# A two-layer decoder trunk on one core: shorter Pool instructions, one head's rotation on DVE, deferred work spread out, two reordered joints

## The chip, the cores and the metric

The kernel runs on 1 core of one Trainium2 chip. The metric is device time in microseconds; 3 runs of the kernel before have a median of 1151.61 us (1150.71 to 1155.07). PE is TensorE, DVE is VectorE, ACT is ScalarE, POOL is GpSimd, SP is SyncE, which issues the DMAs.

## What is computed

The input x is 512 tokens of 1024 features in fp32. Each of two layers computes

```python
n = rmsnorm(h, attn_norm[l])
u, v_sgu, q, k, v_att = split(n @ w_in[l])                # 512 columns each
y_sgu = gelu(u) * (causal_128x128(w_s) @ rmsnorm_by_group(gelu(v_sgu)) + b_s)
y_att = differential_attention(rope(q), rope(k), v_att)   # 4 heads, two softmaxes each, normed
h = h + concat(y_sgu, y_att) @ w_out[l]
h = h + (silu(conv3(n2 @ w_up_gate)) * conv3(n2 @ w_up_value)) @ w_down[l]   # n2 = rmsnorm(h, ffn_norm[l])
```

and a last rmsnorm follows. The FFN has 2816 gate and 2816 value features; conv3 is a causal convolution of width 3 along the tokens.

## The kernel before, in words

**Products.** Features lie on the 128 partitions, the 512 tokens along the free dimension. Each fp32 operand is split into a high part (a cast to fp32r) and a low part (the rest, by a subtraction), and each product is three matmuls: high by high, high by low, low by high. A step of `feat_gemm` (L235) takes one of eight input blocks for two output banks, 6 matmuls of 128x512; `tok_gemm` (L252) does the same with tokens as rows, 12 matmuls of 128x256.

**Weights.** `block` (L156) keeps two blocks ahead (AHEAD): SP issues the DMA of a 128x1024 block into `raw`, ACT casts it into `wh`, and DVE or Pool subtracts (`wl <- raw, wh`, L169 and L170). Pool does nearly all blocks of w_in and w_out and every third of the FFN, DVE the others. Three buffers each hold `raw`, `wh` and `wl`, so the cast of a block waits until TensorE has used up an earlier one. A new block is asked for at every fourth step.

**Order.** From the input products to the end of the attention and of w_out, each engine's instructions are pinned to program order (`pin`, L107). In the FFN they are not; the tile framework orders them. TensorE's products are written as generators; `run(steps, n)` (L261) advances a product by n steps and after each takes one piece of DVE, ACT and Pool work from the queue `due`.

**Input products.** `products` (L770) goes in each layer through gate values, queries and keys of heads 0 and 1, attention values of heads 0 and 1, then queries, keys and values of heads 2 and 3, the gates u, and the first part of w_out. `rope` (L491) rotates two heads: `turn` shuffles on DVE (sh), multiplies by cosines on DVE (t1), multiplies by sines on Pool and adds on Pool; `part` splits the result (ACT cast, DVE subtraction), giving k_0h and k_0l for head 0. The last DVE piece before the attention is `small` (L460): the mixing factor lambda, `nlam`.

**Attention.** 16 units (4 heads by 4 query tiles, L848 to L903), each passing through scores, mask and minimum on DVE (`s<-sc,mask` and `mn`), exponentials on ACT, difference on DVE (`s<-s,cf,s`), transposes (`at`), a split (`aTh` on ACT, `aTl` on DVE), values (`av`) and their sum on DVE (`o<-av`). Units are pipelined: unit i's scores stand beside unit i-1's transposes and unit i-2's values. During the first eight units, three steps of the input products run per unit. Score banks and transpose banks are two each, so scores wait for a mask reduction and `at` or `av` for an earlier `aTl` or `o`. Temporary tiles (t1, sh, score tiles, gate values) share a pool `tp` of 12 buffers. In layer 0 the second gate's norm work is not in `due`: all of it but the first two pieces (squares, sums, square root, normalisations, splits) goes into `later` (L768, L777) and then the masking and split of the spatial weights (`spatial`, L478, L834); up to two entries are taken at each unit's end (L899). Layer 1 has an empty `later`.

**Towards the FFN.** After the attention, w_out's output blocks 0 to 3 (`pairs`) lack their last two inputs; `late` (blocks 4 and 5) begins with six steps, then the last head's output is transposed and split (`end.out_turn`, `out_high`, `out_low`), then `project_last` adds input 6, one step of `late`, `project_last` adds input 7 (L918 to L929). Then come a weight block, the residual of blocks 0 to 3 (`hT<-wo,hT`, which frees their banks, and the next norm's scaled pieces gh_f and gl_f and squares), the rest of `late`, and blocks 6 and 7 in the freed banks. In the FFN's first pair, six of eight gate steps run, then `norm.sums` (L414): TensorE transposes the summed squares acc_f into ss_f, DVE reduces them and takes the reciprocal square root by 11 small operations after one scaling; then the last two gate steps, one value step, `norm.rows` (L424), which transposes the root into rows and copies them to rstd on ACT, and the rest.

Of the kernel before, what the change touches and what calls it, by code (L numbers as in the profile page):

```python
# [13 lines left out]
F32 = mybir.dt.float32  # L14
# [8 lines left out]
S = 512  # L23
# [46 lines left out]
def trunk(ctx: ExitStack, tc, a, out):  # L70
# [50 lines left out]
    pe, act, dve, gps = Ordered(nc.tensor), Ordered(nc.scalar), Ordered(nc.vector), Ordered(nc.gpsimd)  # L121
# [21 lines left out]
    for l in range(DEPTH):  # L143
        specs += [a["w_in"][l, c] for c in range(20)]
        specs += [a["w_out"][l, c] for c in range(8)]
        for half in range(2):
            lo = 0 if half == 0 else FF_SPLIT[0] // 2
# [8 lines left out]
    def block(i):  # L156
        while len(loaded) <= min(i + AHEAD[0], len(specs) - 1):
            j = len(loaded)
            n = specs[j].shape[-1]
            if j >= len(specs) - 6:  # L160
                loaded.append(kept(j, n))
                continue
            raw = wp.tile([P, 1024], F32, tag="raw", name=f"raw{j}")[:, :n]
            h = wp.tile([P, 1024], F32R, tag="wh", name=f"wh{j}")[:, :n]
            lo = wp.tile([P, 1024], F32R, tag="wl", name=f"wl{j}")[:, :n]
            (sync if j < 6 else nc.sync).dma_start(out=raw, in_=specs[j])
            act.copy(h, raw)
            i_l = j % (len(specs) // DEPTH)
            eng = gps if (j > 6 and i_l != 27 if i_l < 28 else j % 3 == 1) else dve  # L169
            eng.tensor_sub(lo, raw, h.bitcast(F32))  # L170
            loaded.append((h, lo))
        return loaded[i]

# [87 lines left out]
    def run(steps, n=None):  # L261

        for i, _ in enumerate(steps):
            if due:
                due.popleft()()
            if i + 1 == n:
                break


    due = deque()  # L270
# [178 lines left out]
    for l in range(DEPTH):  # L449
# [28 lines left out]
        def spatial():  # L478
            gps.affine_select(
                out=wsp, in_=wsp, compare_op=ALU.is_ge, fill=0.0, base=0,  # L480
                pattern=[[0, NG], [1, P]], channel_multiplier=-1,
            )
            act.copy(ws_h, wsp)
            gps.tensor_sub(ws_l, wsp, ws_h.bitcast(F32))

        qs, ks = [None] * NH, [None] * NH
# [4 lines left out]
        def rope(banks, store, at, name):  # L491

            t1, sh = [None, None], [None, None]

            def turn(j):
                sh[j] = tmp(f"{name}{l}_{at + j}sh")
                dve.stream_shuffle(sh[j], banks[j], SHUF)
                t1[j] = tmp(f"{name}{l}_{at + j}t1")
                dve.tensor_mul(t1[j], banks[j], Cr)
                gps.tensor_mul(sh[j], sh[j], Sr)  # L500
                gps.tensor_add(t1[j], t1[j], sh[j])

            def part(j):
                store[at + j] = split(f"{name}{l}_{at + j}", t1[j])

            return [partial(turn, 0), partial(turn, 1), partial(part, 0), partial(part, 1)]

        def query_banks(hp):
            return [mm_bank(f"q{2 * hp + j}_{l}") for j in range(2)]
# [6 lines left out]
        def keys(hp):  # L516
            banks = [mm_bank(f"k{2 * hp + j}_{l}") for j in range(2)]
            yield from feat_gemm(banks, xs)
            due.extend(rope(banks, ks, 2 * hp, "k"))

        def values(hp):
            banks = [mm_bank(f"va{b}_{hp}_{l}") for b in range(2)]
# [241 lines left out]
            g, q = gate_work(0, vb), rope(qb, qs, 0, "q")  # L764
            due.extend([nothing] * 4 + g[:2] + q[:2] + g[2:4] + [lambda: [f() for f in g[4:7]]] + q[2:] + g[7:])


        later = deque()  # L768

        def products():  # L770
            if l == 0:
                yield from both_first()
                banks = value_banks(1, sc_bank)
                yield from tok_gemm(banks, xs)
                g = gate_work(1, banks)
                due.extend(g[:2])
                later.extend(g[2:])  # L777
            else:
                yield from gate_values(0)
                yield from queries(0)  # L780
                yield from gate_values(1)
            yield from keys(0)
            yield from values(0)
            yield from queries(1)
            yield from keys(1)
            yield from values(1)
            yield from gates(0)
            yield from gates(1)
            yield from project()
# [15 lines left out]
        def project_last(k):  # L805
            for c in range(2):
                feat_step(pairs[c], mixed[k], final[0], (2 * c + k - KD + 2) * 256, False, k == KD - 1)
# [3 lines left out]
        steps = products()  # L811
        if l == 0:
# [7 lines left out]
            Cr, Sr = rotary_turn()  # L820
        else:
# [7 lines left out]
            Cr, Sr = fslot(f"Cr{l}"), fslot(f"Sr{l}")  # L829
            dve.tensor_mul(Cr, CT, norm.rstd)  # L830
            dve.tensor_mul(Sr, ST, norm.rstd)
        run(steps, 28 - (22 if l == 0 else 15))
        if l == 0:
            later.append(spatial)  # L834
        else:
            spatial()
        run(steps, 12)
        flush()
# [9 lines left out]
        for i in range(len(todo) + 2):  # L848
            u0 = None
            u1, u2, u3 = at(i - 1), at(i - 2), at(i - 3)  # L850
            ot = at(i - HEAD_LATE)
            if ot and ot.qt < NT - 1:
                ot = None
            if ot:
                ot.out_turn()
                ot.out_high()
            if u3:
                u3.out()
            if biased:
                biased.pop()()  # L860
            if i < len(todo):
                h, qt = todo[i]
                if qt == 0:
                    head = Head(h)
                units.append(Unit(h, qt, head))
                u0 = units[i]
                u0.scores()
            if ot:
                ot.out_low()
            run(steps, 1)  # L870
            if u1:
                u1.turn()
            if u0:
                u0.exps()
            elif i == len(todo):
                gelu(0)
                gelu(1)
            if u3:
                u3.out_square()
                if u3.qt == NT - 1:  # L880
                    u3.out_rms()
            run(steps, 1)
            if u1:
                u1.high()
            if u0:
                u0.difference()
            if u1:
                u1.low()
            n3 = at(i - 4)
            if n3 and n3.qt == NT - 1:  # L890
                n3.out_norm()
            if u2:
                u2.values()
            if i in MIX_AT:
                biased.append(mix(MIX_AT.index(i)))
            for _ in range(min(2, len(later))):
                later.popleft()()
            if i < 8:
                run(steps, 1)  # L899
            if i == len(todo):  # L900
                gated(0)
                gelu(2)
                gelu(3)  # L903
# [14 lines left out]
        late = [sc_bank(f"wo{4 + j}_{l}") for j in range(2)]  # L918
        more = feat_gemm(late, mixed)
        AHEAD[0] = 1  # L920
        run(more, 6)
        AHEAD[0] = 2
        end.out_turn()
        end.out_high()
        end.out_low()
        mixed[-1] = ya[3]
        project_last(KD - 2)
        run(more, 1)
        project_last(KD - 1)  # L929
        flush()  # L930

# [40 lines left out]
        for half in range(2):  # L972
            nf = FF_SPLIT[half]
            acts = []
            for pr in range(nf // 2):
                f = f0 + 2 * pr
                gb = [mm_bank(f"g{f + j}_{l}") for j in range(2)]
                steps = feat_gemm(gb, xs)
                vb = [mm_bank(f"v{f + j}_{l}") for j in range(2)]
                more = feat_gemm(vb, xs)  # L980
                if half == 0 and pr == 0:
                    run(steps, 6)
                    norm.sums()
                    run(steps)
                    run(more, 1)
                    norm.rows()
                run(steps)
                gs = []
                for j in range(2):
                    c = conv(gb[j], f + j, f"cg{l}_{f + j}")  # L990
                    act.activation(c, c, AF.Silu)
                    gs.append(c)
                run(more)
                for j in range(2):
                    c = conv(vb[j], NF + f + j, f"cv{l}_{f + j}")
                    dve.tensor_mul(c, c, gs[j])
                    acts.append(split(f"ac{l}_{f + j}", c, gps))
            f0 += nf
            if half == 1 and not last_layer:
                norm = Norm(f"a{l + 1}", C_AN + (l + 1) * KD)  # L1000
            for c in range(2 if half == 1 and last_layer else 4):
                banks = [mm_bank(f"dn{half}_{2 * c + j}_{l}") for j in range(2)]
                run(feat_gemm(banks, acts))
                if half == 1 and last_layer:

                    block(len(specs) - (4 if c == 0 else 1))
                for j in range(2):
                    m = 2 * c + j
                    dve.tensor_add(hT[m], banks[j], hT[m])
                    if half == 1 and not last_layer:  # L1010
                        norm.feed(m)
# [169 lines left out]
```

## Time and profile before

| what | value |
|---|---|
| median of 3 runs | 1151.61 us |
| the profiled execution's own time | 1152.52 us |
| its span, first to last instruction | 1150.8 us |
| mean granted TensorE clock | 0.993 |
| busy: PE, PEld | 97%, 81% |
| busy: DVE, ACT, POOL | 61%, 41%, 34% |
| chain that ended last: PE, DVE, ACT, POOL | 84%, 7%, 3%, 3% |

The execution's time is the span and 1.7 us around it. PEld is TensorE's weight load, which lies beside its matmuls. The span falls into layer 0's input products and attention (to about 172 us), w_out and the FFN (to 577), the same for layer 1 (to 735 and 1133), and the last norm. In the views below, start and length are in us, "out<-in" are the program's tile names without numbers of buffers, and what stands in brackets is the idle time of that engine just before and who ended it. L119 is the line of the wrapper through which pinned instructions go, so tile names tell them apart.

### The profile page before, as it was taken

Reading aid. Unit: us, or ns where it says so; the run is one execution under the profiler, and the core shown is the slowest. Engines: PE = TensorE matmul, PEld = TensorE weight load, DVE = VectorE, ACT = ScalarE, POOL = GpSimd, SP = SyncE. Lnnn points to the kernel's source line nnn. Section 1 sums busy time; section 2 is a strip of 40 time slices with the busy share of each in tenths; the row PEclk is TensorE's granted clock in tenths of the full one; section 3 lists DMA queues with packets and bytes.
Section 4 is the critical chain, followed back from the end, with each engine's and each line's share of the span. In section 5 each row is a group of like instructions: output and inputs, shape, how many; then the busy total and the mean of one; then the engine's idle time right before and its main releaser. Section 6 shows DMA issues by size and latency. Waiting matters only on the chain.

```text
span 1150.8 us, 14822 instructions
## 1 busy us (share of the span) xinstructions
PE 1119.3 (97%) x5637; PEld 937.6 (81%) x5637; DVE 697.3 (61%) x1267; ACT 477.4 (41%) x810; POOL 393.0 (34%) x303
## 2 busy tenths in 40 slices
PE   9998999999999999999999999999999999999996
PEld 7976887788888888888899688877888888888886
DVE  6778874866663236674357777757666522565634
ACT  6544552454442134343343554544444421344351
POOL 0556223522422013323456652252323311322351
PEclk9999999999999999999999999999999999999998
DMA  8221122223233332233232211222333333232222
GB/s 268 74 74 55 56 65 74 92 92 103 84 107 92 110 92 92 92 101 92 101 106 81 85 59 53 73 74 95 108 92 99 96 99 93 90 110 92 81 85 73
DMA packets 34215, 105.24 MB, mean 91 GB/s; under 512 B 4064, under 2 KB 8544, under 8 KB 34144
## 3 DMA queue, kind: packets, MB, share of 16 engines
q1 hardware_dynamic: 33712, 104.27, 28.6%
q8 instruction: 44, 0.72, 0.3%
q14 instruction: 27, 0.22, 0.1%
q10 hardware_dynamic: 432, 0.03, 0.0%
HBM read 102.19 MB, written 2.10 MB: 91 GB/s over the span
## 4 chain that ended last, share of the span: by engine, by line
PE 84%; DVE 7%; ACT 3%; POOL 3%; issue 2%; DVEq 0%; POOLq 0%; ACTq 0%
PE v L119 21%; PE g L119 20%; PE dn L119 18%; PE wo L119 7%; PE u L119 4%; PE vs L119 3%; PE dl L119 3%; PE q L119 2%; PE k L119 1%; ACT wh L119 1%; PE sc L119 1%; PE av L119 1%; PE mx L119 1%; DVE s L119 1%; POOL wl L119 1%
## 5 line engine op out<-in xcount | busy, mean ns | idle before, releaser
L119 POOL TENSOR_TENSOR wl<-raw,wh 128x1024 fp32r<-128x1024 f32 (+1 forms) x96 | 230.1, 2398 | 580.4 <-ACT wh L119 570.5
L119 ACT CAST wh<-raw 128x1024 fp32r<-128x1024 f32 (+1 forms) x192 | 194.2, 1014 | 376.3 <-issue 189.4
L119 DVE TENSOR_TENSOR wl<-raw,wh 128x1024 fp32r<-128x1024 f32 (+1 forms) x96 | 123.3, 1284 | 135.9 <-ACT wh L119 135.8
L119 PE MATMUL g<-gh_f,wh 128*128 128x512 f32 x352 | 137.8, 391 | 0.0
L119 PE MATMUL g<-gh_f,wl 128*128 128x512 f32 x352 | 137.7, 391 | 0.0
L119 PE MATMUL g<-gl_f,wh 128*128 128x512 f32 x352 | 137.5, 391 | 0.0
L119 PE MATMUL v<-gh_f,wh 128*128 128x512 f32 x352 | 137.1, 390 | 0.0
L119 PE MATMUL v<-gh_f,wl 128*128 128x512 f32 x352 | 137.0, 389 | 0.0
L119 PE MATMUL v<-gl_f,wh 128*128 128x512 f32 x352 | 136.9, 389 | 0.0
L119 DVE SCALAR_TENSOR_TENSOR cv<-up_cv,par,cv 128x512 f32<-128x512 f32 x88 | 74.3, 890 | 7.7 <-ACT cv L119 7.4
L119 PEld LDWEIGHTS g<-gh_f,wh 128*128 128x128 f32 x352 | 66.5, 189 | 13.9
L119 PEld LDWEIGHTS g<-gl_f,wh 128*128 128x128 f32 x352 | 66.5, 189 | 13.8
L119 PEld LDWEIGHTS g<-gh_f,wl 128*128 128x128 f32 x352 | 66.4, 189 | 13.9
L119 PEld LDWEIGHTS v<-gh_f,wh 128*128 128x128 f32 x352 | 66.1, 188 | 13.7
L119 PEld LDWEIGHTS v<-gh_f,wl 128*128 128x128 f32 x352 | 66.1, 188 | 13.7
L119 PEld LDWEIGHTS v<-gl_f,wh 128*128 128x128 f32 x352 | 66.1, 188 | 13.6
L119 DVE SCALAR_TENSOR_TENSOR cg<-up_cg,par,cg 128x512 f32<-128x512 f32 x88 | 71.1, 855 | 6.8 <-ACT cg L119 6.3
L119 DVE TENSOR_TENSOR up_cv<-v,rstd_f 128x512 f32<-128x512 f32 x44 | 30.2, 692 | 67.6 <-PE v L119 67.6
L119 ACT ACTIVATE s<-s,mn 128x128 f32<-128x128 f32 (+3 forms) x64 | 35.5, 556 | 66.5 <-DVE mn L119 66.5
L119 DVE TENSOR_TENSOR up_cg<-g,rstd_f 128x512 f32<-128x512 f32 x44 | 30.0, 692 | 54.1 <-PE g L119 53.5
L119 DVE TENSOR_TENSOR hT<-dn,hT 128x512 f32<-128x512 f32 x28 | 19.1, 690 | 47.8 <-PE dn L119 47.8
L119 ACT ACTIVATE cg<-cg 128x512 f32<-128x512 f32 x44 | 27.7, 630 | 46.6 <-DVE cg L119 46.6
(604 smaller groups left out, 2625.7 us busy)
## 6 DMA issues: line engine op xcount, KB each, us to landing
raw<-in_w_up SPq DMA_DIRECT2D x88, 512.0 KB, 3.4
raw<-in_w_dn SPq DMA_DIRECT2D x40, 512.0 KB, 3.5
raw<-in_w_in SPq DMA_DIRECT2D x36, 512.0 KB, 3.4
raw<-in_w_out SPq DMA_DIRECT2D x16, 512.0 KB, 3.4
hT<-in_xT SPq DMA_DIRECT2D x8, 256.0 KB, 4.4
or<-in_w_in SPq DMA_DIRECT2D x16, 128.0 KB, 4.1
raw<-in_w_dn SPq DMA_DIRECT2D x8, 256.0 KB, 3.2
out<-y SPq DMA_DIRECT2D x8, 256.0 KB, 2.2
```

Of the source, the lines that this page charges most:

```text
L119: return lambda *args, **kw: pin(getattr(self.engine, op)(*args, **kw))
```

## The change

It runs Pool's weight subtractions as two of 512 columns; puts the product and sum of head 0's keys on DVE in both layers; moves the split of head 1's keys from `due` to the front of `later`, so that it comes at the end of the first attention unit; takes one entry of `later` per unit instead of two, with the spatial weights and both squares of the second gate as one entry (now the second of nine); runs all eight gate steps before the FFN norm's sums and three value steps before its rows; and runs five steps of `late` before the last head's transposes, a sixth after them, then both `project_last`, leaving two steps for after the residual.

```diff
             eng = gps if (j > 6 and i_l != 27 if i_l < 28 else j % 3 == 1) else dve
-            eng.tensor_sub(lo, raw, h.bitcast(F32))
+
+            for c in range(0, n, S) if eng is gps else (0,):
+                c = slice(c, min(n, c + S) if eng is gps else n)
+                eng.tensor_sub(lo[:, c], raw[:, c], h.bitcast(F32)[:, c])
...
                 dve.tensor_mul(t1[j], banks[j], Cr)
-                gps.tensor_mul(sh[j], sh[j], Sr)
-                gps.tensor_add(t1[j], t1[j], sh[j])
+                eng = dve if name == "k" and at + j == 0 else gps
+                eng.tensor_mul(sh[j], sh[j], Sr)
+                eng.tensor_add(t1[j], t1[j], sh[j])
...
+        later = deque()
...
             yield from feat_gemm(banks, xs)
-            due.extend(rope(banks, ks, 2 * hp, "k"))
+            turned = rope(banks, ks, 2 * hp, "k")
+            if hp == 0:
+
+                later.appendleft(turned.pop())
+            due.extend(turned)
...
-        later = deque()
-
...
-                later.extend(g[2:])
+                later.extend([lambda: (spatial(), g[2](), g[3]())] + g[4:])
...
-        if l == 0:
-            later.append(spatial)
-        else:
+        if l > 0:
             spatial()
...
-            for _ in range(min(2, len(later))):
+            if later:
                 later.popleft()()
...
-        run(more, 6)
+        run(more, 5)
         AHEAD[0] = 2
         end.out_turn()
         end.out_high()
         end.out_low()
         mixed[-1] = ya[3]
+        run(more, 1)
         project_last(KD - 2)
-        run(more, 1)
         project_last(KD - 1)
...
                 if half == 0 and pr == 0:
-                    run(steps, 6)
+                    run(steps)
                     norm.sums()
-                    run(steps)
-                    run(more, 1)
+                    run(more, 3)
                     norm.rows()
```

## Rows read from the trace of the kernel before

**Rows 1.** The page's first part: busy us (share) and instructions.

```profile
PE 1119.3 (97%) x5637; PEld 937.6 (81%) x5637; DVE 697.3 (61%) x1267; ACT 477.4 (41%) x810; POOL 393.0 (34%) x303
```

**Rows 2.** TensorE's waits, 60 to 105 us: us in total, times, longest.

```profile
PE av L119 <- DVE o L119: 3.8, 2, 2.3
PE at L119 <- DVE aTl L119: 1.8, 1, 1.8
PE sc L119 <- DVE k_0l L119: 0.9, 1, 0.9
PE at L119 <- DVE s L119: 0.8, 1, 0.8
PE sc L119 <- DVE mn L119: 0.6, 1, 0.6
```

**Rows 3.** TensorE's waits, 580 to 670 us (layer 1).

```profile
PE sc L119 <- DVE mn L119: 0.9, 1, 0.9
PE sc L119 <- DVE k_0l L119: 0.8, 1, 0.8
```

**Rows 4.** TensorE's waits, 195 to 580 us (758 to 800 shows the same two).

```profile
PE ss_f L119 <- DVE acc_f L119: 2.4, 1, 2.4
PE wo L119 <- DVE hT L119: 1.5, 1, 1.5
```

**Rows 5.** Two stretches: us, busy PE, PEld, DVE, ACT, POOL, then PEclk, DMA, GB/s.

```profile
97.92:101.33 3.41, 3.17 (x11) 2.81 (x12) 2.55 (x11) 2.68 (x9) 0.51 (x2) 0.50 0.51 154
224.21:227.62 3.41, 3.41 (x9) 2.64 (x9) 2.44 (x13) 0.00 (x0) 0.00 (x0) 0.50 0.37 137
```

**Rows 6.** Timeline, 82 to 98 us, Pool and DVE.

```profile
83.22 2.39 POOL L119 TENSOR_TENSOR wl<-raw,wh 128x1024 fp32r<-128x1024 f32 x1 [4.14 <-ACT wh L119]
...
83.39 2.77 DVE L119 TENSOR_TENSOR vs<-vs,gr 128x512 f32<-128x512 f32 x1
...
93.64 0.68 DVE L119 TENSOR_TENSOR vs<-vs,gr 128x512 f32<-128x512 f32 x1
```

**Rows 7.** Timeline, 44.2 to 48.5 us, Pool and DVE.

```profile
44.29 1.29 POOL L119 TENSOR_TENSOR q_1t<-q_1t,q_1sh 128x512 f32<-128x512 f32 x1
44.34 1.79 DVE L119 TENSOR_TENSOR q_0l<-q_0t,q_0h 128x512 fp32r<-128x512 f32 x1
...
45.54 5.21 POOL L119 TENSOR_TENSOR wl<-raw,wh 128x1024 fp32r<-128x1024 f32 x2
```

**Rows 8.** Timeline, head 0's keys: layer 0 (two rows), layer 1 (the last).

```profile
59.36 1.30 POOL L119 TENSOR_TENSOR k_0sh<-k_0sh,sr 128x512 f32<-128x512 f32 x1 [1.30 <-DVE k_0sh L119]
...
62.72 2.21 DVE L119 TENSOR_TENSOR k_0l<-k_0t,k_0h 128x512 fp32r<-128x512 f32 x1 [1.63 <-ACT k_0h L119]
...
628.44 2.42 POOL L119 TENSOR_TENSOR wl<-raw,wh 128x1024 fp32r<-128x1024 f32 x1 [3.83 <-ACT wh L119]
```

**Rows 9.** TensorE's waits, 105 to 195 us: the longest of four.

```profile
PE ot L119 <- DVE aTl L119: 0.6, 1, 0.6
```

**Rows 10.** Two stretches of layer 0's attention, columns as in rows 5.

```profile
85.00:92.00 7.00, 5.51 (x28) 3.72 (x26) 7.00 (x17) 3.22 (x9) 5.44 (x5) 1.00 0.25 75
102.00:117.00 15.00, 15.00 (x118) 13.65 (x119) 11.30 (x32) 6.45 (x18) 9.92 (x7) 1.00 0.12 37
```

**Rows 11.** Timeline, DVE: the first and last of twelve small operations.

```profile
224.72 0.17 DVE L421 TENSOR_SCALAR ss_f<-ss_f 128x4 f32<-128x4 f32 x1
...
226.91 0.16 DVE L386 SCALAR_TENSOR_TENSOR rcol_f<-rcol_f0t,rcol_f 128x4 f32<-128x4 f32 x1
```

**Rows 12.** Timeline, DVE: the last addition of squares.

```profile
220.35 2.83 DVE L119 TENSOR_TENSOR acc_f<-acc_f,sq_f 128x512 f32<-128x512 f32 x1
```

**Rows 13.** Chain of waits: eight gate steps (start, us).

```profile
239.70 10.88 PE g L119 x48
```

**Rows 14.** Timeline, 197 to 202 us: a weight block ahead of the residual.

```profile
198.52 1.05 ACT L119 CAST wh<-raw 128x1024 fp32r<-128x1024 f32 x1 [5.91 <-PE wo L119]
...
199.66 1.22 DVE L119 TENSOR_TENSOR wl<-raw,wh 128x1024 fp32r<-128x1024 f32 x1 [6.27 <-ACT wh L119]
```

## The prediction

> **What bounds the kernel now.** I read the busy shares first: the TensorE matmul row covers 97% of the span of 1150.8 us [rows 1], so a change can win only the time in which TensorE waits or runs at its lower clock. No matmul is added or removed here. Second, TensorE's waits, stretch by stretch. Every one of them names DVE. Layer 0 from 60 to 105 us (last key products and first attention units): 3.8 + 1.8 + 0.9 + 0.8 + 0.6 = 7.9 us [rows 2]. The same stretch of layer 1: 0.9 + 0.8 = 1.7 us in the two that count [rows 3]. The way from the attention into the FFN: 2.4 us for the norm's sum and 1.5 us for the residual, in each layer [rows 4]. Third, the granted clock: it falls to 0.50, the level of 1.2 GHz, for 3.41 us after the longest waits of layer 0, at 97.92 and at 224.21 us; TensorE is busy for 3.17 and 3.41 us of these [rows 5], so work that takes half as long at 2.4 GHz costs another 1.6 and 1.7 us.
>
> Why DVE is late can be read in the timeline. An addition or multiplication of 128x512 with both operands in SBUF takes 0.68 us while Pool is idle, but 2.77 us when Pool has begun a weight subtraction of 2.39 us just before it; it ends 0.55 us after Pool's instruction does [rows 6]. So such a DVE instruction sits out whatever Pool has in hand, and all that is queued on DVE behind it sits out too.
>
> **Part 1, the subtraction in halves.** Pool's long instruction becomes two of 512 columns. The nearest row is Pool's product of that size, 1.30 us [rows 8]; two make 2.60, 0.2 us more than the 2.39. What DVE can lose in one meeting falls from about 2.1 us to about 1.0. This holds only if DVE gets in between two queued Pool instructions. It does: behind Pool's q_1t (44.29, 1.29 us) stood a waiting DVE subtraction and Pool's own next one. DVE ended at 46.13, 0.55 us after q_1t, and Pool's two following subtractions took 5.21 us instead of 2 x 2.39 [rows 7]. So I take halves to let DVE in; that Pool runs on from half to half stays a rival with a small chance. (The Trainium skill's page GPSIMD Engine Reference, section 2.1 Instruction dispatch, says that consecutive Pool instructions are no barrier, each Pool core starting its share of the next as soon as it has ended its own. By that rule two queued halves could run on as one and open nothing; the trace shows an opening of 0.43 us in the 5.21.)
>
> Alone, the halves touch the smaller waits of both attention stretches, the longest 0.6 us, four in layer 0 [rows 9] and four alike in layer 1. That is at most 2.4 us per layer; against it stand 0.2 us more Pool time per block and the work that part 3 puts there. I take 0.5 us in all; ends -1 and 3.4. In the FFN TensorE waits for nothing, so there I cost the halves at 0; the cover is the two blocks that the weights run ahead.
>
> **Part 2, the first head's keys.** Before, the product and the sum of head 0's keys stood on Pool behind a weight subtraction; in layer 0 the last DVE piece, k_0l, started at 62.72 and took 2.21 us because the next subtraction had begun [rows 8]. TensorE waits for it (0.9, in layer 1 0.8), then for the mask reduction mn (0.6 and 0.9), which is queued on DVE behind head 1's split, and in layer 0 for s (0.8). After, DVE does both operations (two of 0.68 us), Pool is rid of 2.6 us, and head 1's split goes to the end of the first unit; head 1 is read four units later. In layer 0, DVE's shuffle ends just ahead of Pool's start at 59.36 [rows 8]; its product, DVE's two new operations, the cast (some half of the 1.05 us that one of 1024 columns takes [rows 14]) and the split, 0.68 each, end by 62.6 when none meets a Pool instruction and by about 64 when two do. TensorE comes at 62.72 + 2.21 - 0.9 = 64.0. All 2.3 us go. In layer 1 the shuffle comes while Pool is in a subtraction that began at 628.44 [rows 8]: product, sum and split can each sit out a half of 1.3 us, then k_0l is as late as before. So of 0.8 + 0.9 I take 1.2, ends 0 and 1.7. The sum of the part: 3.5 us.
>
> **Part 3, the deferred work.** In layer 0, two pieces of the second gate's work were taken per unit; now one, with the spatial weights and both squares together in the second unit. From 85 to 92 us DVE is busy for 7.00 of 7.00 us; from 102 to 117 for 11.30 of 15.00, and there TensorE never idles [rows 10]. The change carries two normalisations and two splits, each 0.68 us or up to 2.8 when it meets Pool, from the full stretch into the next, where 3.7 us are free. The twelve small operations of the square root (from 224.72 to 227.07 where the FFN's norm does the same twelve, 2.35 us [rows 11]) go to the end of the fifth unit, just ahead of that stretch. The waits aimed at are av and at, 3.8 + 1.8 = 5.6 us, and the clock's 1.6. Layer 1 does the same units without deferred work and has no wait there that reaches those of [rows 3]; with one sum of 0.68 us per unit left in layer 0, I leave 1.0 us standing: 4.6 + 1.6 = 6.2 us. Ends: 2.8, if half of the waits stays and with them the low clock, and 7.2, if all goes.
>
> **Part 4, FFN norm sums after eight steps instead of six.** A step is 10.88 / 8 = 1.36 us [rows 13]. TensorE comes to the sums 2.72 us later and waited 2.4; acc_f began at 220.35 and took 2.83 [rows 12] because Pool was in a weight subtraction, so with halves it is earlier, if anything. The two steps moved ahead of the sums read pieces that DVE wrote before acc_f, and TensorE reaches them at about 220.8 (the end of acc_f less the wait). Nothing else is passed: no weight block is asked for within them, so no DMA moves. The rows follow three steps behind the sums as before: 4.1 us, against 1.5 from the end of acc_f to the first small operation and 2.35 for the twelve, 3.9. The new distance is from the rows to the next use of their banks, five steps or 6.8 us instead of seven; a copy and two products of 512 columns, some 0.7 each by [rows 6], need about 2. One thing comes nearer: the first value step's weight block, whose DVE split (1.22 us, like the one of [rows 14]) is asked for right behind the sums. Ordered ahead of the square root it would make the chain 5.1 and a new wait of 1.0 in front of the rows. I take the program's order, so the wait goes in both layers, 4.8 us, and with it the low clock at 224.21, 1.7: 6.5 us. Ends: 2.8, if the new wait comes and the low clock stays, and 6.5.
>
> **Part 5, the wo steps.** The chain is: the last product of the pairs frees a weight buffer, ACT casts the next block (198.52, 1.05 us), DVE splits it (199.66, 1.22), then adds the residual (0.68 by [rows 6]), which frees TensorE's bank at 201.5 [rows 14]. One step of 1.36 us covered it; now two do. 1.5 - 1.36 leaves 0.1: 1.36 us per layer, 2.7 in all, 3.0 if nothing is left. Both weight blocks are still asked for within the five steps that stay, so the prefetch does not move. The last head's transposes come 1.36 us earlier; no wait for them is in the rows now, so they could cost at most 1.36 per layer, which is the low end, 0 for the part; I take no cost, since none of the waits seen names them.
>
> **The sum.** 0.5 + 3.5 + 6.2 + 6.5 + 2.7 = 19.4 us off the profiled execution's own 1152.5 us: 1133.1. The median of the runs, 1151.6, lies 0.9 below that execution, which I leave inside the range. The low ends of the terms give -1 + 2.3 + 2.8 + 2.8 + 0 = 6.9 us or 1145.6; the high ends 3.4 + 4.0 + 7.2 + 6.5 + 3.0 = 24.1 or 1128.4.
>
> **The rivals.** First, the attention waits only move on: with TensorE earlier DVE becomes what ends last from 57 to 105 us. For it: 7.00 of 7.00 busy; against it: part of that is blocked time, which the change cuts. Half of parts 2 and 3 (9.7 us) comes back: 1138.0. Second, Pool runs on from half to half without letting DVE in: part 1 turns from 0.5 into -0.5, and each of the three DVE operations in layer 1's key chain sits out a whole subtraction, which takes the 1.2 away; 1135.3. Against it: the opening of [rows 7]; for it: that opening is one meeting among many. Third, the change does not do what it says: the FFN is not pinned to program order, and the sums may stay where they were. Then part 4's 6.5 is missing: 1139.6. Fourth, slower: the tmp pool has 12 buffers, and the gate's two value tiles now live until the ninth unit instead of the fifth, beside three score tiles, four of the key rotation and two head outputs. I count 11. If a thirteenth were asked for, a unit's mask reduction would wait for a rotation to end, four Pool operations of 1.30 behind a subtraction of 2.39, 7.6 us, in each of units 5 to 8, and each could bring the low clock (1.7) as the 2.4 before the sums did: 4 x 9.3 = 37.2 us, 1170.3. It decides from the thirteenth live tile on; nothing in the waits now points to the pool.
>
> **How the numbers follow.** Forecast 0.70, moved waits 0.17, halves as one 0.06, sums unmoved 0.04, buffers 0.03. The first four, and the low ends together (6.9 us), are below before by more than 0.5% (5.8 us, about what a measurement of this kernel can tell from no change). Leaving 0.03 for a rival on top of low ends, within 0.5%, faster has 0.94, slower 0.03. The range 1128 to 1140 runs from the high ends to the third rival and leaves out the buffers and the lowest ends.
>
> **What would show it.** Pool's subtractions about 1.3 us, two per block; DVE operations beside them at most 2 us. No wait on ss_f; the one on hT at most 0.3; k_0l gone in layer 0 and at most 0.8 in layer 1; av and at together at most 1 in 60 to 105; clock 1.00 at both places. Wrong would be: TensorE waits of the same sum at other places (first rival), DVE operations of 2.8 us still beside two halves (second), sums still ahead of step seven (third), or waits of several us in units 5 to 8 (fourth).

## The result, and the profile after

The changed kernel took 1135.6 us, the median of four runs (1135.21 to 1136.36); the kernel before took 1152.18 beside it. The ratio is 0.9854, 95% interval 0.9833 to 0.9874: faster by 1.5%. The forecast was 1133.1 us with a range of 1128 to 1140. The profiled execution has a span of 1134.6 us against 1150.8: 16.2 us of the 19.4 forecast came.

The page's first part and its row of the clock, answering [rows 1]:

```profile
PE 1115.3 (98%) x5637; PEld 935.4 (82%) x5637; DVE 687.8 (61%) x1271; ACT 478.4 (42%) x810; POOL 412.6 (36%) x390
...
PEclk9999999999999999999999999999999999999998
```

Pool has 87 instructions and 19.6 us more, DVE is busy 9.5 us less. TensorE's waits after the change, in four stretches (60 to 105, 105 to 195, 195 to 580 and 580 to 670 us, parted by the dots; us in total, times, longest):

```profile
PE at L119 <- DVE aTl L119: 2.0, 2, 1.9
...
PE at L119 <- DVE aTl L119: 2.1, 2, 1.7
PE av L119 <- DVE or_3t L387: 1.1, 1, 1.1
PE ot L119 <- DVE aTl L119: 0.6, 1, 0.6
PE ot L119 <- DVE cf L692: 0.2, 1, 0.2
...
PE sr_f L119 <- DVE rcol_f L389: 0.2, 1, 0.2
...
PE at L119 <- DVE aTl L119: 0.5, 1, 0.5
PE sc L119 <- DVE k_0l L119: 0.3, 1, 0.3
```

Against [rows 2 to 4] and [rows 9]: the sums' wait and the residual's wait are gone in the FFN, the keys' wait is gone in layer 0 and 0.3 in layer 1, and the 7.9 us of the first attention units are 2.0. But 105 to 195 us, which had four short waits, now has 4.0 us, two of them of 1.7 and 1.1.

Where the microseconds came from is read best by the start of the same TensorE instruction in each profiled execution: the first `wo` of layer 0 (163.35 us before), the first scores of layer 1 (634.20), the first `wo` of layer 1 (725.87) and the first product of the last norm (1110.50). Each column is what was gained from one mark to the next, in us, against before:

| kernel | layer 0 to its first `wo` | to layer 1's scores | to layer 1's first `wo` | to the last norm | median of runs |
|---|---|---|---|---|---|
| forecast | 8.75 | 5.46 | 1.45 | 3.76 | 1133.1 |
| changed kernel | 5.47 | 5.21 | 1.82 | 3.66 | 1135.6 |
| halves alone | 3.07 | 3.94 | -0.28 | 2.61 | 1143.39 |
| keys alone | -0.46 | 1.59 | 2.02 | -1.40 | 1152.11 |
| spread alone | 2.15 | 0.00 | -0.09 | -1.61 | 1151.79 |
| joints alone | -0.27 | 5.28 | -0.10 | 3.67 | 1142.74 |
| halves and joints | 3.01 | 4.99 | -0.36 | 3.65 | 1141.48 |
| changed, whole subtractions | 3.58 | 5.26 | 1.96 | 3.69 | 1138.05 |

(The forecast's row is its own terms put on the stretches: 2.3 + 6.2 + half of the 0.5; 1.36 + 2.4 + 1.7; 1.2 and the other half; 1.36 + 2.4.) Each row of a kernel is one profiled execution, so a stretch in which the clock fell in one of the two kernels and not in the other moves by some 1.6 us for that alone. Three stretches came within 0.4 us of the forecast. All that is missing in sum, 3.3 us, is missing in layer 0's attention.

### The profile page after: what moved, and what is told of

The parts are those of the page before. It is cut to its first block, busy times and chain, and to the rows that moved or that the text cites. A ratio compares the mean times of both kernels' runs of the same rounds, so it can differ in the third digit from the quotient of the medians.

```text
span 1134.6 us, 14944 instructions
## 1 busy us (share of the span) xinstructions
PE 1115.3 (98%) x5637; PEld 935.4 (82%) x5637; DVE 687.8 (61%) x1271; ACT 478.4 (42%) x810; POOL 412.6 (36%) x390
## 4 chain that ended last, share of the span: by engine, by line
PE 85%; DVE 9%; ACT 3%; POOL 2%; issue 1%; DVEq 0%; ACTq 0%; POOLq 0%
PE g L119 21%; PE v L119 21%; PE dn L119 19%; PE wo L119 7%; PE u L119 4%; PE vs L119 3%; PE q L119 3%; PE dl L119 3%; PE sc L119 1%; ACT wh L119 1%; DVE s L119 1%; PE mx L119 1%; PE av L119 1%; POOL wl L119 1%; ACT s L119 1%
## 5 line engine op out<-in xcount | busy, mean ns | idle before, releaser
L119 POOL TENSOR_TENSOR wl<-raw,wh 128x512 fp32r<-128x512 f32 x187 | 255.4, 1387 | 567.2 <-ACT wh L119 556.4
```

The lines of the kernel that those rows point to most:

```text
L119: return lambda *args, **kw: pin(getattr(self.engine, op)(*args, **kw))
```

## The experiments: each part alone

**Halves alone.** The kernel before with this edit and nothing else:

```diff
-            eng.tensor_sub(lo, raw, h.bitcast(F32))
+            for c in range(0, n, S) if eng is gps else (0,):
+                c = slice(c, min(n, c + S) if eng is gps else n)
+                eng.tensor_sub(lo[:, c], raw[:, c], h.bitcast(F32)[:, c])
```

> The kernel before with Pool's subtractions in halves, nothing else. If halves let DVE in, DVE operations that meet one take at most 2.0 us instead of 2.77, and the waits of layer 0 from 60 to 105 us (7.9) shrink by 1 to 3 us: 1149 to 1151. If Pool runs on from half to half, DVE operations of 2.7 us stay and the time is 1152 to 1153.

Measured: 1143.39 us, ratio 0.9917 (0.9901 to 0.9934), a gain of 9.5 us. Its waits from 60 to 105 us and then from 195 to 580 us:

```profile
PE at L119 <- DVE aTl L119: 2.0, 1, 2.0
PE av L119 <- DVE o L119: 1.8, 2, 1.3
PE at L119 <- DVE s L119: 1.0, 1, 1.0
PE sc L119 <- DVE mn L119: 0.9, 1, 0.9
...
PE wo L119 <- DVE hT L119: 1.5, 1, 1.5
```

The keys' wait of layer 0 is gone, and so is the wait for the FFN's sum: the last addition of squares, which took 2.83 us behind a whole subtraction [rows 12], starts at 216.16 and takes 0.68:

```profile
216.16 0.68 DVE L119 TENSOR_TENSOR acc_f<-acc_f,sq_f 128x512 f32<-128x512 f32 x1
...
216.17 3.07 POOL L119 TENSOR_TENSOR wl<-raw,wh 128x512 fp32r<-128x512 f32 x2 [1.10 <-ACT wh L119]
```

It met no half here: it started 0.01 us ahead of Pool's next two, because the two `gl_f` before it, beside an earlier block, took 3.27 us (from 206.03) and not 4.38 as before (from 209.10). So the halves by themselves win what part 4 was given, the low clock with it, and 3 us in layer 0's attention, where the clock now stays at 1.00 too: about half of the 3 us is the low clock's, which the prediction gave to part 3. That Pool lets DVE in between two halves can be read in the changed kernel's timeline (start, us, engine, operation; Pool's two halves are one row):

```profile
56.14 3.00 POOL L119 TENSOR_TENSOR wl<-raw,wh 128x512 fp32r<-128x512 f32 x2 [4.51 <-ACT wh L119]
...
56.62 1.37 DVE L119 TENSOR_TENSOR vg_1l<-vs,vg_1h 128x512 fp32r<-128x512 f32 x1 [0.78 <-ACT vg_1h L119]
...
58.55 0.67 DVE L119 TENSOR_TENSOR k_0t<-k,cr 128x512 f32<-128x512 f32 x1
59.14 0.68 DVE L119 TENSOR_TENSOR k_0sh<-k_0sh,sr 128x512 f32<-128x512 f32 x1
```

The split begins beside the first half and ends after 1.37 us, while the second half is still running (Pool ends at 59.14); before, such an operation took 2.77 [rows 6]. The Trainium skill (GPSIMD Engine Reference, 2.1 Instruction dispatch) says that consecutive Pool instructions are no barrier between Pool's cores. Whether the two halves ran on in that way no row shows; DVE was not kept out by it, as the 1.37 us show.

**Keys alone.**

```diff
-                gps.tensor_mul(sh[j], sh[j], Sr)
-                gps.tensor_add(t1[j], t1[j], sh[j])
+                eng = dve if name == "k" and at + j == 0 else gps
+                eng.tensor_mul(sh[j], sh[j], Sr)
+                eng.tensor_add(t1[j], t1[j], sh[j])
...
+            turned = rope(banks, ks, 2 * hp, "k")
+            if hp == 0:
+                later.appendleft(turned.pop())
+            due.extend(turned)
```

> The kernel before with head 0's keys rotated on DVE and head 1's split deferred. If the parts add, the waits k_0l, mn and s go (2.3 us in layer 0, 1.2 to 1.7 in layer 1): about 1148.5. Rival: DVE is what ends last in layer 0 up to 100 us, TensorE only comes earlier to the waits for o and aTl there, and layer 0 gives its 2.3 back: 1150.5 to 1151.

Measured: 1152.11 us, ratio 0.9994 (0.9982 to 1.0006): nothing. The timeline of layer 0's keys, Pool and DVE:

```profile
59.35 2.41 POOL L119 TENSOR_TENSOR wl<-raw,wh 128x1024 fp32r<-128x1024 f32 x1 [1.21 <-ACT wh L119]
...
59.84 2.46 DVE L119 TENSOR_TENSOR k_0sh<-k_0sh,sr 128x512 f32<-128x512 f32 x1
...
64.18 1.41 DVE L119 TENSOR_TENSOR k_0l<-k_0t,k_0h 128x512 fp32r<-128x512 f32 x1
```

The product moved to DVE meets the whole subtraction that Pool, now free, begins at 59.35. It takes 2.46 instead of 0.68, and k_0l starts 1.5 us later than before [rows 8]. In the changed kernel the same product takes 0.68 (59.14 above), but not beside a half: the split ahead of it is over sooner (1.37 us; 2.49 here), so it starts as Pool ends, and 0.86 us before Pool's next block (60.00). Further on this kernel has waits of 3.3 and 3.4 us for aTl, and the clock falls behind each (0.89 on average from 90 to 105 and from 105 to 120 us). In layer 1, where the product stood behind such a subtraction on Pool before as well (628.44 in [rows 8]), the part does give 2.02 us; 1.40 are lost again 60 us on, to the clock (below). So the medians' "nothing" seems to be a sum of gains and low clocks: the ten runs lie between 1149.49 us (mean clock 0.994) and 1154.94 (0.987), and the one in the table, 1150.77, is 1.8 us below the profiled execution before.

**Spread alone.**

```diff
-                later.extend(g[2:])
+                later.extend([lambda: (spatial(), g[2](), g[3]())] + g[4:])
...
-            for _ in range(min(2, len(later))):
+            if later:
                 later.popleft()()
```

> The kernel before with one deferred entry per unit and the spatial weights beside both squares. If the parts add, the waits for o and aTl from 85 to 98 us (5.6) fall to about 1 and the low clock there goes: 1146. Rival: the entry with the spatial weights holds ACT and the square root holds DVE later on, so half comes back as waits for aTl: about 1149.

Measured: 1151.79 us, ratio 0.9988 (0.9979 to 0.9997). Layer 0's attention gains 2.15 us: the two waits for `o` are gone, but 1.3 for the square root (94.3 us), 1.0 for aTl (112) and 1.4 for the head's root (115) are new. Then 1.61 us go in the second FFN, which the edit does not touch: there the clock falls after the sums' wait, as it did not before. The stretches are this kernel's behind that wait, and the same of the kernel before (us, busy PE, PEld, DVE, ACT, POOL, then PEclk, DMA, GB/s):

```profile
785.20:788.60 3.40, 3.40 (x10) 2.61 (x10) 1.97 (x12) 0.00 (x0) 0.00 (x0) 0.60 0.23 94
```

```profile
787.20:790.60 3.40, 3.40 (x17) 2.74 (x16) 2.40 (x13) 1.05 (x1) 0.00 (x0) 1.00 0.26 105
```

**Joints alone.**

```diff
-        run(more, 6)
+        run(more, 5)
...
+        run(more, 1)
         project_last(KD - 2)
-        run(more, 1)
...
-                    run(steps, 6)
+                    run(steps)
                     norm.sums()
-                    run(steps)
-                    run(more, 1)
+                    run(more, 3)
```

> The kernel before with the FFN norm's sums after eight steps and the wo steps reordered. If the parts add, no wait on ss_f, at most 0.2 on hT, and no low clock behind them: 2 x 2.4 + 2 x 1.4 + 1.7 = 9.3 us, 1143. Rival: without halves the last sum of squares is later, and some 1 us per layer of wait stays: 1145.

Measured: 1142.74 us, ratio 0.9909 (0.9895 to 0.9924). From 195 to 580 us the waits are now one row:

```profile
PE sr_f L119 <- DVE rcol_f L386: 0.2, 1, 0.2
```

5.28 us in the first FFN and 3.67 in the second, against 5.46 and 3.76 forecast. Parts 4 and 5 held in size. One step of part 4 did not: it took the program's order on DVE, the square root ahead of the next weight block's split. In both layers, with every kernel here that has this edit, the split came first; in the changed kernel:

```profile
217.92 1.21 DVE L119 TENSOR_TENSOR wl<-raw,wh 128x1024 fp32r<-128x1024 f32 x1
219.05 0.16 DVE L424 TENSOR_SCALAR ss_f<-ss_f 128x4 f32<-128x4 f32 x1
```

The prediction had priced that order at 1.0 us in front of the rows; it cost the 0.2 of the row above, since TensorE was busy for 4.7 us from the start of the sums (216.67) to the end of the three steps, not for 4.1. Halves and joints win the same wait of the sums, so their gains alone (9.5 and 10.2) don't add.

## The experiments: what the parts are worth together

**Whole subtractions in the changed kernel** (the halves undone, everything else kept):

```diff
-            for c in range(0, n, S) if eng is gps else (0,):
-                c = slice(c, min(n, c + S) if eng is gps else n)
-                eng.tensor_sub(lo[:, c], raw[:, c], h.bitcast(F32)[:, c])
+            eng.tensor_sub(lo, raw, h.bitcast(F32))
```

> The changed kernel with Pool's subtractions whole again. If the halves are worth the 0.5 us of the forecast: 1136 to 1136.5. If they carry part of what the other edits win, because less deferred work leaves the meetings with Pool as what makes DVE late: waits of layer 0 up to 120 us of 6 us or more instead of 5.3, and 1138 or more.

Measured: 1138.05 us, ratio 0.987 (0.9856 to 0.9885), so with the rest in place the halves are worth 2.4 us. The first row of its waits from 60 to 105 us names the keys again:

```profile
PE sc L119 <- DVE k_0l L119: 1.5, 1, 1.5
```

Behind that wait the clock falls in the profiled execution (0.54 from 66.7 to 70.1 us), which by [rows 5] costs some 1.6 us: most of the 1.9 by which layer 0's attention is longer than in the changed kernel may be the clock's. The fastest of the four runs, with a mean clock of 0.998, still took 1137.66.

**Halves and joints** (the first and the fourth diff together).

> The kernel before with the halved subtractions, the norm sums two steps later and the reordered wo steps; without the keys on DVE and without the thinner deferred work. Theory B (waits of layer 0's attention move on, so that keys and spread are worth little even beside the halves): layer 0's waits from 60 to 120 us sum to about 5.7 us as with the halves alone, against 5.0 in the changed kernel; layer 1 keeps its 0.8 for k_0l; 1137 to 1138.5 us. Theory of the prediction (keys 3.5 and spread 4.6 of their own): 1142 to 1144 us.

Measured: 1141.48 us, ratio 0.9902 (0.9887 to 0.9917), between the two and nearer to the prediction's 1142. Layer 0's waits are those of the halves alone, as theory B had them, but layer 1's are worse than it had allowed for (580 to 680 us):

```profile
PE sc L119 <- DVE mn L119: 1.6, 3, 1.1
PE at L119 <- DVE aTl L119: 1.0, 2, 0.5
PE sc L119 <- DVE k_0l L119: 0.8, 1, 0.8
```

Set beside the changed kernel, keys and spread are worth 2.5 us in layer 0's attention and 2.2 in layer 1's once the halves are there; by the medians 5.9 in all, where parts 2 and 3 had 8.1 without the low clock. No run has the halves with only one of the two, so how the 5.9 are shared stays open.

## The experiments: can the rest go?

The theory at this point was that in layer 0's attention DVE, with the time it sits out behind Pool, is what ends last, so that a wait taken away comes back behind it. Its rival: the two places of the changed kernel that still wait are faults of order, each with a remedy. The timeline of the wait at 87.5 us, ACT, Pool and DVE:

```profile
76.46 0.62 ACT L119 CAST wsh<-wsp 128x512 fp32r<-128x512 f32 x1 [3.08 <-POOL wsp L119]
...
87.10 1.60 POOL L119 TENSOR_TENSOR q_3t<-q_3t,q_3sh 128x512 f32<-128x512 f32 x1
...
87.49 1.75 DVE L119 SCALAR_TENSOR_TENSOR s<-s,cf,s 128x512 f32<-128x512 f32 x1
89.17 0.55 DVE L119 TENSOR_TENSOR aTl<-at,aTh 128x384 fp32r<-128x384 f32 x1
```

ACT stands for 3.08 us until Pool has masked the spatial weights, and that unit's exponentials come behind it; later the difference `s` sits out Pool's rotation. Five kernels move the deferred work; each replaces this line of the changed kernel (`g[2:4]` the squares, `g[4:6]` their sums, `g[6]` the root, `g[7:9]` the normalisations, `g[9:]` the splits; one entry per unit):

```diff
-                later.extend([lambda: (spatial(), g[2](), g[3]())] + g[4:])
```

**Spatial weights apart**, in the fifth unit:

```diff
+                later.extend([lambda: (g[2](), g[3]())] + g[4:6] + [lambda: (spatial(), g[6]())] + g[7:])
```

> The changed kernel with the spatial weights moved from the squares (second unit) to the square root (fifth unit). Theory: the wait of 1.9 us for aTl at 88 us comes from ACT, which stands 3 us in front of unit 2's exponentials waiting for Pool's masking of the spatial weights; apart it falls to layer 1's 0.5 and the time by about 1.3. Rival: it is the rotation of heads 2 and 3 on Pool behind the weight halves, and stays at 1.5 or more, the time within 0.3.

Measured: 1136.08 us, ratio 0.9852 (0.9834 to 0.9869). The wait at 87 us falls from 1.9 to 0.4, as the remedy had it; a wait of 1.6 for aTl appears at 94, behind the root's first operations (from 89.38).

**Root late**, in the eighth unit instead of the fifth:

```diff
+                later.extend([lambda: (spatial(), g[2](), g[3]())] + g[4:6] + [nothing] * 3 + g[6:])
```

> The changed kernel with the square root and what follows it three units later (units 8 to 12). Theory: the new waits at 108 to 113 us (1.7 for aTl, 1.1 for or) come from the square root's small operations and the first normalisation, which hold DVE in units 5 and 6, and so Pool's rotation of the keys; without them the stretch is like layer 1's, with at most 0.5 left: 1133. Rival: the rotation of the keys on Pool is late by itself once TensorE is early, and 2 us or more stay: 1135 to 1136.

Measured: 1136.35 us, ratio 0.9854 (0.9839 to 0.9869). The wait for or_3t is gone; aTl's at 108 is 1.3 instead of 1.7, and waits for mn (0.5) and, at 138, for aTl (0.5) are new. But the root itself did not move: its operations start at 90.99 us here and at 91.16 in the changed kernel, both times behind the second sum of squares (the reason is under the root in the tenth unit). Only normalisations and splits came later, so this run does not test whether the root makes the wait at 108.

**Both late:**

```diff
+                later.extend([nothing] * 3 + [spatial, g[2], lambda: (g[4](), g[3]()), g[5], g[6], lambda: (g[7](), g[9]()), g[8], g[10]])
```

> The changed kernel with nothing deferred in units 2 to 4, the spatial weights in unit 5 and the second gate's squares, sums, root, normalisations and splits in units 6 to 12. If both theories hold, waits of layer 0 from 60 to 115 us are at most 1.2 instead of 5: about 1131.5. Rival: DVE has no room in units 9 to 12 either, and 1 to 3 us of waits appear from 120 to 150 us: 1133 to 1136.

Measured: 1136.25 us, ratio 0.9855 (0.984 to 0.9871). Between 60 and 105 us only 0.4 is left; then one wait of 2.9 comes at 116. Its row, and DVE's timeline there:

```profile
PE ot L119 <- DVE gr_1t L387: 2.9, 1, 2.9
...
115.07 1.20 DVE L384 TENSOR_SCALAR gr<-gs 128x8 int32<-128x8 int32 x1
...
117.81 0.16 DVE L389 SCALAR_TENSOR_TENSOR gr<-gr_1t,gr 128x8 f32<-128x8 f32 x1
117.89 0.87 DVE L119 SCALAR_TENSOR_TENSOR va<-va,rcol_a,va 128x256 fp32r<-128x256 f32 x2
```

The root's small operations stand ahead of the low halves `va`, which free the bank that the output transposes need. Here squares, sums and root did leave their place ahead of 96 us, and the wait at 108 is gone. In the changed kernel it can be followed back to DVE through Pool: Pool's block ahead of the rotation of heads 2 and 3's keys waits for DVE (here it starts at 95.61), and DVE later waits for head 2's keys:

```profile
99.25 3.00 POOL L119 TENSOR_TENSOR wl<-raw,wh 128x512 fp32r<-128x512 f32 x2 [5.95 <-DVE s L119]
...
105.55 1.11 DVE L119 TENSOR_TENSOR k_2l<-k_2t,k_2h 128x512 fp32r<-128x512 f32 x1 [1.94 <-ACT k_2h L119]
```

**The root in the tenth unit:**

```diff
+                later.extend([nothing] * 3 + [spatial, g[2], lambda: (g[4](), g[3]()), g[5], nothing, g[6]]
+                             + [lambda: (g[7](), g[9]()), lambda: (g[8](), g[10]())])
```

> The changed kernel with nothing of the deferred work in units 2 to 4, the spatial weights in unit 5, the squares, sums and the root after them, the root at the end of unit 10 (behind that unit's output transposes) instead of ahead of unit 9's low halves. Theory A (the root's order on DVE made the 2.9 us wait, and the rest of layer 0's attention has room): no wait over 0.6 us in 60 to 125 us, clock 1.00, about 1131.5 us. Theory B (DVE is what ends last in layer 0's attention, every relief moves the wait): another wait of 1 to 3 us behind unit 10, 1134.5 to 1136 us, no different from the changed kernel's 1135.6.

Measured: 1138.33 us, ratio 0.9877 (0.986 to 0.9893), and the same wait of 2.9 for the same reason. The edit did not move what it was to move: the root is not held to the program's order (`nc.vector`, not the pinned `dve`), and here it again stands one operation behind the second sum of squares (`gs` at 113.64, the root from 114.57), though a later unit calls it.

**Sum and root in the tenth unit:**

```diff
+                later.extend([nothing] * 3 + [spatial, g[2], lambda: (g[4](), g[3]()), nothing, nothing, lambda: (g[5](), g[6]())]
+                             + [lambda: (g[7](), g[9]()), lambda: (g[8](), g[10]())])
```

> As the run with the root at the end of unit 10, but the second sum of squares goes with it. The root's operations are not held to the order they are written in: they were placed on DVE right behind that second sum, wherever the root was called, so that run had the same wait of 2.9 us as the one before it. Now sum and root stand behind the unit's low halves of the values on DVE, so the output transposes do not find their bank taken. Theory A (the order of the root made that wait): the 2.9 us go, what is left from 60 to 125 us is 0.4 + 0.3 + 0.5, and with the 2 us that normalisations and splits may cost next, 1131.5 to 1133.5 us. Theory B (DVE ends last all through layer 0's attention and the wait moves on): the 2.9 us come back as one or two waits between 118 and 145 us, 1134.5 to 1136.5 us.

Measured: 1136.44 us, ratio 0.9864 (0.9847 to 0.988). Its waits from 60 to 150 us, and the stretch behind the new one (columns as above):

```profile
PE sc L119 <- DVE mn L119: 2.1, 3, 1.5
PE at L119 <- DVE aTl L119: 0.9, 2, 0.5
PE av L119 <- DVE or_3t L388: 0.5, 1, 0.5
...
135.50:138.90 3.40, 3.40 (x14) 2.62 (x12) 2.80 (x7) 1.20 (x5) 0.00 (x0) 0.56 0.00 0
```

The 2.9 us for `ot` are gone, and 0.5 + 1.5 us for the next head's root and the next mask come at 132 to 134.5, with a low clock behind them. That is what the theory had forecast. In all five placements layer 0's first `wo` starts between 157.54 and 158.15 us; in the changed kernel, at 157.88. None of them is better than the changed kernel.

**Quarters:**

```diff
-            for c in range(0, n, S) if eng is gps else (0,):
-                c = slice(c, min(n, c + S) if eng is gps else n)
+            for c in range(0, n, S // 2) if eng is gps else (0,):
+                c = slice(c, min(n, c + S // 2) if eng is gps else n)
```

> The changed kernel with Pool's subtractions in four pieces of 256 columns instead of two of 512. Theory (a blocked DVE instruction sits out the one Pool instruction that is running, so its length sets the loss): Pool's pieces take about 0.7 us each, 2.8 per block, DVE's blocked instructions of 512 columns fall from about 1.4 to 1.75 us to about 1.2 to 1.4 us, layer 0's waits lose 1 to 2 us in all: 1133.5 to 1135 us. Rival (what is lost is DVE's time in total, not in one meeting; four openings only mean four meetings and Pool runs later): the same waits, Pool's blocks 0.3 us longer, 1135.5 to 1137 us.

Measured: 1135.79 us, ratio 0.9853 (0.9838 to 0.9868), the rival. Pool's group in the list by lines (count, busy us, mean ns):

```profile
L119 POOL TENSOR_TENSOR wl<-raw,wh 128x256 fp32r<-128x256 f32 x364 | 295.0, 841 | 535.0 <-ACT wh L119 521.1 <-DVE s L119 5.5 <-PE av L119 4.5
```

A piece takes 0.84 us, a block 3.4, where two halves of 1387 ns take 2.8. The waits for aTl at 87 and 108 us stay, 2.0 each. Here making the meeting shorter pays at two pieces; at four Pool's own time goes up and nothing more is gained.

## Why the prediction was right, and where it was not

**The direction, the FFN, the wo steps** (parts 4 and 5) were right in size as well: 9.2 us forecast, and the two FFN stretches gave 5.21 + 3.66 = 8.9, with the joints alone 5.28 + 3.67. The wait on the residual fell to a gap of 0.1 us, the one on the sums to nothing. Two steps failed without harm to the sum. The weight block's split did come ahead of the square root, which the prediction had ruled out, and cost 0.2 us of its 1.0: the order was misjudged, and it was luck that the price was too high. And part 1 wins the sums' wait as well: "In the FFN TensorE waits for nothing, so there I cost the halves at 0" overlooked its own [rows 4] and [rows 12]. The 1.7 of the low clock in layer 0 came too, but whether the kernel before falls to it there is a matter of the execution (last section).

**Part 2** held in size. Layer 0's k_0l wait went, layer 1's whole attention gained 1.82 us where 1.45 was forecast, with 0.3 left for k_0l. In layer 0 the way there was another: the halves alone took the k_0l wait away, and the part alone made k_0l later.

**Part 1 and part 3 together** are the step that failed. They were to give, with part 2's 2.3, 8.75 us in layer 0's attention, and all three gave 5.47. The term that was mis-sized is part 3's "I leave 1.0 us standing": 2.0 were left in 60 to 105 us, and 2.8 came new at 108 to 113, the very stretch of which the prediction said that 3.7 us were free. Free time of DVE there was in sum, not where TensorE's next transposes wanted it: this row is the changed kernel from 110.2 to 113.6 us (columns as above), TensorE 2.30 of 3.40 and DVE 3.33.

```profile
110.20:113.60 3.40, 2.30 (x18) 2.13 (x19) 3.33 (x7) 0.00 (x0) 2.58 (x2) 1.00 0.00 0
```

Much of that 3.33 is not work. Two small operations of the head's root sit out Pool's halves there, 0.94 and 1.23 us where their neighbours take 0.16, and the wait of 1.1, put down to or_3t, ends right behind them:

```profile
109.75 3.03 POOL L119 TENSOR_TENSOR wl<-raw,wh 128x512 fp32r<-128x512 f32 x2 [1.95 <-ACT wh L119]
...
110.11 0.94 DVE L388 TENSOR_TENSOR or_3t<-or_3t,or 128x4 f32<-128x4 f32 x1
...
111.57 1.23 DVE L389 SCALAR_TENSOR_TENSOR or<-or_3t,or 128x4 f32<-128x4 f32 x1
```

The prediction had sized such meetings for operations of 128x512 alone.

The step also left out a wait that the change adds: with spatial weights and squares in one entry, ACT stands behind Pool's masking (3.08 us above), ahead of exponentials. And within the sum of 8.75 the shares were wrong: the halves, given 0.25 there, gave 3.1 by themselves, low clock included, and keys and spread, given 8.5, gave 2.5 on top. That the stretch came out no further off is luck: the halves made up for about half of what parts 2 and 3 fell short.

**The rivals.** The first, attention waits that only move on, is what happened in part, at 3.3 us instead of its 4.9; five placements of the deferred work, all ending within 0.6 us of each other, show that waits move. That DVE, with the time it sits out, is the reason is read from waits that all name DVE and stretches like the one above, and from the wait at 108, which went when sums and root stood later, with one of 2.9 us in their new place. No run left the deferred work out, so it isn't shown that the stretch would then be free. The second fell (1.37 us at 56.62 and 1.80 at 61.70 beside two halves; no operation of 128x512 took 2.8). The third fell: the sums moved. The fourth fell: no wait of several microseconds in units 5 to 8, the longest there being the 1.7. The clock is at full level (1.00) at both places of [rows 5].

## What to carry to other kernels

Where two engines block each other, size a shorter instruction by all places where the other one is late, not by the stretch that is being looked at; here cutting Pool's subtraction in two was worth 9.5 us alone and 2.4 beside edits that win the same waits, and cutting it in four nothing more. Moving a short operation from Pool to DVE did not pay where Pool, now free, began its next long instruction over it. Deferred work that is spread into a stretch needs gaps between deadlines, not free time in sum: look for the instruction that stands just ahead of what TensorE asks for next, and for what it sits out there. And see in the trace that a moved instruction has moved: those outside the pinned order stayed where their inputs became ready.

## What was not expected

The sums' wait of 2.4 to 2.5 us lowered the clock behind it in layer 0 and not in layer 1 in the kernel before, in both layers with the spread alone (0.57 at 221.80 and 0.60 at 785.20), and with the keys alone in layer 1 only (0.74 at 784.00; 1.00 at 224.50). In the same program it seems to go either way: of the kernel with the root in the tenth unit, the profiled execution had a clock of 1.00 behind its wait of 2.9 us and took 1136.29 us, the other three took 1137.9 to 1139.15 at a mean clock of 0.994 or 0.995 instead of 0.997; where in these three the clock fell, no trace shows. So a gain of one low clock, 1.6 us, may be counted only with a chance.
Small operations sit out Pool, too: besides the two above, `gr`, 128x8, took 1.20 us at 115.07 in the run with both late, against 0.17 for its neighbours.
